# The second feed-forward product by Strassen's seven block products, with its rows kept in HBM

## The chip, the cores and the metric

One core of a Trainium2 chip runs the whole kernel. The metric is the time of one execution on the device in microseconds (us), as the median of several runs. For one more execution there is a profile taken by the hardware profiler, with a trace of every instruction. TensorE multiplies matrices, VectorE and ScalarE work on whole tiles, GpSimd is a slower general engine that can also issue DMAs, and SyncE issues DMAs.

## The reference

One layer of a hybrid decoder for 1024 prompt rows and 8 sample rows, so 1032 rows of 1024 channels. After the mixer (projections, short convolution, state-space scan) and a first LayerNorm comes the feed-forward part, which is all that the change touches:

```
v = x * (1 + sc2) + sh2
hid = jnp.square(jax.nn.relu(jnp.einsum('bld,df->blf', v, w_up)))
x = layer_norm(ALPHA * x + (1 + g2) * jnp.einsum('blf,fd->bld', hid, w_down), ln2_g, ln2_b)
```

`w_up` is 1024 x 4096 and `w_down` 4096 x 1024, in float32. `g2` depends on the channel, and for the sample rows also on the row.

## The kernel before, in words

Everything lies transposed: a tile has 128 channels on the partitions and the 1032 rows along the free dimension. The hidden layer has 4096/128 = 32 such tiles, and the output has 8 (`x1[0]` to `x1[7]`, in SBUF).

Each float32 operand is split into a high part in fp32r and a low part (what the high part leaves), by a cast on ScalarE and a subtraction on VectorE (`split`, line 201). A product of two such operands takes three matmuls: high by high, low by high, high by low (`term`, line 204). `product` (line 212) makes one output tile from a list of operand tiles: for each of the three blocks of 344 rows it runs all terms into one PSUM bank and then calls an eviction. Line 210 is the matmul of every such product.

`hidden(i)` (line 949) makes hidden tile i from the eight tiles of v: 3 x 8 x 3 = 72 matmuls; its eviction is ReLU on ScalarE, a square on VectorE and the split (lines 944 and 945). The tiles are taken in five groups of four (`NFA`, line 985) and two of six (`NFB`, line 1002). After each group the down product adds what the group gives to all eight output tiles: for each of them, 3 blocks by 4 (or 6) hidden tiles by 3 matmuls, evicted by `gate_add` (line 786), one VectorE operation that multiplies PSUM by the gate and adds it to `x1[m]` in SBUF (line 789), with two small operations for the 8 sample rows (lines 792 and 793). In the last group the LayerNorm is worked in: the down product runs over blocks of 392, 384 and 256 rows (`LAST`), and statistics, normalisation and stores of one block lie beside the matmuls of the next.

Weights come in tiles of 512 KB (384 KB in the groups of six) through SyncE's queue, in the order of the list `order`, always one ahead of the tile in use, into two `raw` buffers, and are split into `whi` and `wlo`. The tile framework places each instruction in its engine's queue by a simulated schedule, puts in the semaphore waits, and hands out the buffers by tag. PSUM has four banks for products (`psm`) and three for small results (`pss`). GpSimd issues no DMA in this kernel; its descriptor space is set to 1024 bytes per partition (line 1188).

Of the kernel before, what the change touches and what calls it, by code (L numbers as in the profile page):

```python
# [10 lines left out]
F32 = mybir.dt.float32  # L11
# [6 lines left out]
P = 128  # L18
# [33 lines left out]
SLOTS = {"raw": 2, "whi": 2, "wlo": 2, "G": 2, "xg": 2, "yc": 2}  # L52


NFB = 2
NFA = (DFF // P - 6 * NFB) // 4

# [5 lines left out]
def cols(ap, b):  # L65
    return ap[:, b[0]:b[1]]


def build(tc, ctx, a):
# [23 lines left out]
    def tmp(w=T, dt=F32):  # L93
        return sp.tile([P, w], dt, tag="t", name=nm("t"), bufs=5)
# [46 lines left out]
    def part(tag, dt, w):  # L141
        return sp.tile([P, w], dt, tag=tag, name=nm(tag), bufs=SLOTS.get(tag, 1))
# [6 lines left out]
    def parts(raw, tags, w):  # L149
        hi, lo = (part(t, F32R, w) for t in tags)  # L150
        for ins, first in zip(split(raw, hi, lo), queue):
            after(ins, first)
        return hi, lo
# [8 lines left out]
    for b in range(NB):  # L162
        for m in range(8):
            if b and m % 2 == 0:
                continue
            order.append(("wout", 1, m) + ((("raw", f"S{m}", f"S{m + 1}"),) if m % 2 == 0 else ()))
    for f in range(NFA):
        order += [("wup", i) + ((("raw", "aw", "yt"),) if i == 2 else ()) for i in range(4 * f, 4 * f + 4)]
        order += [("wda", f, mp) for mp in range(4)]
    spare = [f"U{i}" for i in range(8, 14)] + ["C0", "C1", "C2", "C3", "G", "G"]  # L170
    for f in range(NFB):
        order += [("wup", 4 * NFA + 6 * f + i) for i in range(6)]
        for m in range(8):
            tags = ("raw", spare[2 * m - 4], spare[2 * m - 3])
            order.append(("wdb", f, m) + ((tags,) if f == NFB - 1 and m > 1 else ()))
    ahead = []

    queue = []
# [9 lines left out]
    def prefetch():  # L188
        if order:
            key, raw = load_next()  # L190
            ahead.append((key, parts(*raw)))

    def weights(*key):
        if not ahead:
            prefetch()
        got, w = ahead.pop(0)
        assert got == key, (got, key)
        prefetch()
        return w
# [12 lines left out]
    def product(w, ks, evac, blocks=BLOCKS):  # L212
        for b in blocks:
            ps = psm()
            for i, x in enumerate(ks):
                term(ps, w, x, i, len(ks), b)
            evac(b, ps[:, :b[1] - b[0]])
            if not quiet[0]:
                next(background, None)
# [499 lines left out]
    def pair(tags):  # L719
        return [slab(t, F32R) for t in tags]  # L720
# [228 lines left out]
    def hidden(i):  # L949
        w, evac, hl, _ = hidden_start(i)  # L950
        product(w, kv, evac)
        return hl
# [29 lines left out]
    for k in range(8):  # L982
        after(rescale(k, b), vcopy)

    for f in range(NFA):
        kh = [t[2] for t in two] if f == 0 else []
        kh += [hidden(4 * f + i) for i in range(len(kh), 4)]
        for mp in range(4):
            w = weights("wda", f, mp)
            for m in (2 * mp, 2 * mp + 1):  # L990
                product(w, [(4 * (m % 2) + i, h, l) for i, (h, l) in enumerate(kh)],
                        lambda b, ps: gate_add(x1[m], ps, M_G2, m, b))

    def row_shift():

        near, base = tmp(dt=F32R), tmp()
        nc.scalar.copy(near, x1[0])
        for b in BLOCKS:
            ln1.total(base, (cols(near, b),), P, b, w=rones)
        return base  # L1000

    for f in range(NFB):
        if f == NFB - 1:
            base = row_shift()
        kh = []
        for i in range(6):
            kh.append(hidden(4 * NFA + 6 * f + i))
            if f == NFB - 1:
                for m in ((0, 1), (2, 3, 4), (5, 6, 7), (), (), ())[i]:
                    tc.keep_in_program_order(tt(x1[m], x1[m], base, op=ALU.subtract))  # L1010
        kf = [(i, h, l) for i, (h, l) in enumerate(kh)]
        if f < NFB - 1:
            for m in range(8):
                product(weights("wdb", f, m), kf, lambda b, ps: gate_add(x1[m], ps, M_G2, m, b))
            continue
        total = ln1.total
        mean, rsum, qsum = (slab(t) for t in ("xg", "xg", "yc"))
        sq = {}

        def square(m, b):  # L1020
            sq[m] = cols(qsum if m == 0 else tmp(), b)
            act(sq[m], cols(x1[m], b), AF.Square)

        def add_x(m, b):
            s = cols(rsum, b)
            tt(s, s if m > 1 else cols(x1[0], b), cols(x1[m], b), op=ALU.add)

        def add_q(m, b):
            tt(cols(qsum, b), cols(qsum, b), sq[m], op=ALU.add)

        def moments(b, xs=(), qs=()):

            mu, s, q = cols(mean, b), cols(rsum, b), cols(qsum, b)
            total(mean, (s, *(cols(x1[m], b) for m in xs)), D, b)
            act(s, mu, AF.Square)
            total(qsum, (q, *(sq[m] for m in qs)), D, b, eps)

        def variance(b):
            s, q, w = cols(rsum, b), cols(qsum, b), cols(tmp(), b)
            tt(s, q, s, op=ALU.subtract)  # L1040
            act(q, s, AF.Ln)
            act(q, q, AF.Exp, scale=-0.5)
            act(w, q, AF.Square)
            return w

        def newton(b, w):
            s, q = cols(rsum, b), cols(qsum, b)
            stt(w, w, -0.5, s, op0=ALU.mult, op1=ALU.mult)
            stt(q, w, 1.5, q, op0=ALU.add, op1=ALU.mult)

        def center(m, b):
            tt(cols(x1[m], b), cols(x1[m], b), cols(mean, b), op=ALU.subtract)

        def affine(m, b, to):
            tt(cols(x1[m], b), cols(x1[m], b), cols(qsum, b), op=ALU.mult)  # L1055
            if m % 3 == 2:
                nc.gpsimd.tensor_scalar(to, cols(x1[m], b), vc(V_G2, m), vc(V_B2, m), op0=ALU.mult, op1=ALU.add)  # L1057
            else:
                act(to, cols(x1[m], b), AF.Identity, scale=vc(V_G2, m), bias=vc(V_B2, m))

        def output(m, b):
            affine(m, b, cols(x1[m], b))
            dma(a["o_y"][m, :, b[0]:b[1]], cols(x1[m], b))

        wd = []

        def down(m, b):
            product(wd[m], kf, lambda b, ps: gate_add(x1[m], ps, M_G2, m, b), (b,))
            square(m, b)

        b = LAST[0]
        for m in range(8):
            wd.append(weights("wdb", f, m))
            down(m, b)
            if m:
                add_x(m, b)
                add_q(m, b)
        moments(b)

        with tc.manual_schedule(engines={mybir.EngineType.DVE}):  # L1080
            for i in (1, 2):
                b, p, last = LAST[i], LAST[i - 1], i == 2
                for m in range(8):
                    down(m, b)
                    if m == 0:
                        center(0, p)
                        center(1, p)
                        w = variance(p)
                    elif m == 1:
                        center(2, p)  # L1090
                        newton(p, w)
                    else:
                        add_x(m - 1, b)
                        if not last or m < 7:
                            add_q(m - 1, b)
                        if m == 2:
                            output(0, p)
                            output(1, p)
                        elif m < 7:
                            center(m, p)  # L1100
                            output(m - 1, p)
                if not last:
                    add_x(7, b)
                    center(7, p)
                    add_q(7, b)
                    moments(b)
                    output(6, p)
                    output(7, p)
            moments(b, (7,), (6, 7))
            y = [tmp(4 * (b[1] - b[0])).rearrange("p (m c) -> p m c", m=4) for i in range(2)]  # L1110
            output(6, p)
            center(7, p)
            output(7, p)
            for m in range(3):
                center(m, b)
            w = variance(b)
            for m in range(3, 6):
                center(m, b)
            newton(b, w)
            for m in range(8):  # L1120
                if m > 5:
                    center(m, b)
                affine(m, b, y[m // 4][:, m % 4])
                if m % 2:
                    dma(a["o_y"][m - 1:m + 1, :, b[0]:b[1]].rearrange("m p c -> p m c"), y[m // 4][:, m % 4 - 1:m % 4 + 1])
# [81 lines left out]
```

## Time and profile before

| what | value |
|---|---|
| median of 3 runs | 1575.5 us (1573.29 to 1575.7) |
| the profiled execution's own time | 1574.45 us |
| its span, first to last instruction | 1572.6 us |
| mean granted TensorE clock | 0.994 of full speed |
| instructions | 23959, of them 10058 matmuls |

A share is an engine's busy time over the span. The predicted and the measured time are of a whole execution; the rows are all of the profiled one.

### The profile page before, as it was taken

To read this page: it belongs to the slowest core of one execution; us is meant where nothing else is said; L and a number is where in the kernel's file an instruction comes from. 1 tells how busy PE (TensorE), PEld (TensorE's weight loads), DVE (VectorE), ACT (ScalarE), POOL (GpSimd) and SP (SyncE) were. 2 spreads that over 40 slices of the span, in tenths; PEclk is the share of its full clock that TensorE was granted. 3 is DMA by queue.
4 is the path that set the end of the run, shared out by engine and by line. 5 is a ranking of instruction groups with operands and counts; after the bars stand their busy time and mean duration, and the time that the engine had idled before them with its cause. 6 is when DMAs were issued, how large, how long until landed. Compare 5 with 4: busy or idle time off the path is not lost.

```text
span 1572.6 us, 23959 instructions
## 1 busy us (share of the span) xinstructions
PE 1541.8 (98%) x10058; PEld 1489.2 (95%) x10058; DVE 868.6 (55%) x1653; ACT 526.3 (33%) x805; POOL 169.0 (11%) x168
## 2 busy tenths in 40 slices
PE   6999999999999999999999999999999999999996
PEld 5899999999889999999999999999999999999995
DVE  4575556677876742636996444434343433335477
ACT  2553323323333353613577121121312213113334
POOL 0004222221211311100241000000000000000001
PEclk9999999999999999999999999999999999999998
DMA  9332344344343323412221111111111111111102
GB/s 366 114 118 94 108 132 141 118 140 132 135 151 128 119 96 108 175 42 93 82 68 54 41 54 41 48 47 42 53 41 54 41 54 34 45 56 51 61 31 88
DMA packets 49628, 141.44 MB, mean 90 GB/s; under 512 B 5736, under 2 KB 14696, under 8 KB 49520
## 3 DMA queue, kind: packets, MB, share of 16 engines
q1 hardware_dynamic: 49520, 139.91, 27.4%
q8 instruction: 79, 1.29, 0.3%
q14 instruction: 29, 0.24, 0.1%
HBM read 126.33 MB, written 13.56 MB: 89 GB/s over the span
## 4 chain that ended last, share of the span: by engine, by line
PE 94%; DVE 3%; DMA 1%; ACT 1%; issue 1%; POOL 0%; SPq 0%; ACTq 0%; DVEq 0%; POOLq 0%
PE mm L210 86%; PE ada L229 2%; PE sm L651 1%; PE sm L643 1%; PE sm L842 1%; PE sm L638 1%; PE sm L673 1%; PE sm L210 1%; DMA S<-in_xT 0%; PE sm L617 0%; DVE U L1055 0%; PE sm L236 0%; DMA s<-in_ssm 0%; PE sm L597 0%; PE mm L425 0%
## 5 line engine op out<-in xcount | busy, mean ns | idle before, releaser
L210 PE MATMUL mm<-U,whi 128*128 128x344 f32 x3058 | 778.5, 323 | 4.6 <-ACT U L336 4.6
L210 PEld LDWEIGHTS mm<-U,whi 128*128 128x128 f32 x3058 | 536.6, 188 | 21.4 <-issue 11.8
L210 PE MATMUL mm<-U,wlo 128*128 128x344 f32 x1529 | 488.1, 322 | 0.0
L202 ACT CAST whi<-raw 128x1024 fp32r<-128x1024 f32 (+1 forms) x122 | 125.7, 1030 | 544.0 <-PE mm L210 529.8
L210 PEld LDWEIGHTS mm<-U,wlo 128*128 128x128 f32 x1529 | 286.9, 188 | 3.0 <-issue 2.8
L789 DVE SCALAR_TENSOR_TENSOR U<-mm,mod,U 128x344 f32<-128x344 f32 (+3 forms) x216 | 122.7, 571 | 206.5 <-PE mm L210 206.5
L210 PE MATMUL mm<-S,whi 128*128 128x344 f32 (+3 forms) x912 | 232.8, 320 | 0.0
L202 DVE TENSOR_TENSOR wlo<-raw,whi 128x1024 fp32r<-128x1024 f32 (+1 forms) x122 | 146.5, 1201 | 132.2 <-ACT whi L202 131.8
L210 PEld LDWEIGHTS mm<-S,whi 128*128 128x128 f32 x912 | 160.6, 188 | 0.3
L210 PE MATMUL mm<-S,wlo 128*128 128x344 f32 (+3 forms) x456 | 145.3, 320 | 0.0
L210 PE MATMUL mm<-C,whi 128*128 128x344 f32 x516 | 143.0, 320 | 0.0
L944 DVE TENSOR_TENSOR t<-t 128x344 f32<-128x344 f32 x96 | 49.3, 515 | 87.5 <-ACT t L944 87.5
L210 PEld LDWEIGHTS mm<-C,whi 128*128 128x128 f32 x516 | 92.9, 188 | 0.1
L210 PEld LDWEIGHTS mm<-S,wlo 128*128 128x128 f32 x456 | 85.6, 188 | 0.1
L1057 POOL TENSOR_SCALAR U<-U,vec 128x392 f32<-128x392 f32 (+1 forms) x4 | 5.6, 1388 | 720.0 <-DVE U L1055 720.0
L210 PE MATMUL mm<-C,wlo 128*128 128x344 f32 x258 | 82.5, 320 | 0.0
L210 PE MATMUL mm<-G,whi 128*128 128x344 f32 x258 | 82.1, 321 | 0.1
L210 PE MATMUL mm<-xg,whi 128*128 128x344 f32 x258 | 82.0, 320 | 0.0
L387 DVE SCALAR_TENSOR_TENSOR t<-t,vec,t 128x1064 f32<-128x1064 f32 (+1 forms) x52 | 71.8, 1388 | 10.7 <-ACT t L385 9.7
L944 ACT ACTIVATE t<-mm 128x344 f32<-128x344 f32 x96 | 43.6, 455 | 97.0 <-PE mm L210 97.0
L210 PE MATMUL mm<-yc,whi 128*128 128x344 f32 x210 | 66.8, 322 | 0.0
L945 DVE TENSOR_TENSOR S<-t,S 128x344 fp32r<-128x344 f32 x66 | 33.9, 516 | 29.6 <-ACT S L944 29.3
(360 smaller groups left out, 2117.7 us busy)
## 6 DMA issues: line engine op xcount, KB each, us to landing
raw<-in_win SPq DMA_DIRECT2D x44, 512.0 KB, 3.7
aw<-in_wada SPq DMA_DIRECT2D x33, 512.0 KB, 4.2
raw<-in_wup SPq DMA_DIRECT2D x32, 512.0 KB, 3.5
raw<-in_wout SPq DMA_DIRECT2D x24, 512.0 KB, 3.5
raw<-in_wda SPq DMA_DIRECT2D x20, 512.0 KB, 3.5
G<-acd SPq DMA_DIRECT2D x16, 512.0 KB, 3.9
raw<-in_wdb SPq DMA_DIRECT2D x16, 384.0 KB, 3.1
S<-in_xT SPq DMA_DIRECT2D x8, 516.0 KB, 10.2
```

Source lines behind the costliest of these rows:

```text
L202: return nc.scalar.copy(thi, src), tt(tlo, src, thi, op=ALU.subtract)
L210: mm(ps[:, :b[1] - b[0]], wt, cols(xt, b), start=(i == 0 and q == 0), stop=(i == n - 1 and q == 2))
L229: mm(ps[32 * g:32 * g + 32, :256], cs[:, 2 * kp + k2, :], w[:, c:c + 256], start=(kp == 0), stop=(kp == KD // 2 - 1), tile_position=(0, 32 ...
L387: stt(r, t[:, k:k + n], wt(k), r, op0=ALU.mult, op1=ALU.add)
L638: mm(po[:, i * P:(i + 1) * P], st[:, h0:h0 + P], bc[2 + g][:, sl], start=True, stop=True)
L643: mm(py[r * HD:(r + 1) * HD, i * P:(i + 1) * P], xg[g][:, 0, h * HD:(h + 1) * HD], Gs[g][:, h, :], start=True, stop=True, tile_position=(0 ...
L651: mm(pst, bt[:, g * P:(g + 1) * P], xg[g][:, 1], start=True, stop=True)
L673: mm(pn[:, :BW], w, cols(src, b), start=(i == 0), stop=(i == len(srcs) - 1))
L789: stt(dst[:, lo:hi], ps[:, :hi - lo], mod[:, row + m, 0:1], dst[:, lo:hi], op0=ALU.mult, op1=ALU.add)
L842: mm(pn, w, src, start=(i == 0), stop=(i == len(srcs) - 1))
L944: return [lambda: act(x, ps, AF.Relu), lambda: tt(x, x, x, op=ALU.mult), lambda: nc.scalar.copy(xh, x), lambda: tt(xl, x, xh, op=ALU.subtr ...
L945: lambda: tt(xl, x, xh, op=ALU.subtract)]
```

## The change

Tiles 0 to 5 of the hidden layer go through the down product as a group of six before, into `x1` in SBUF; each `x1[m]` is then stored to a buffer `x1d[m]` in HBM. Tiles 26 to 31 are the last group of six, as before. The 20 tiles between them are taken in five groups of four. For a group, the down product of one pair of output tiles is a 2 x 2 block product: two pairs of hidden tiles by two output tiles by two sets of rows (the 1032 rows are seen as quarters of 258, and a set is two of them). It is computed by seven block products in place of eight, in Strassen's form as Winograd gave it: sums of weight blocks (`seven_parts`) and sums of hidden blocks (`operands`) are formed in SBUF by VectorE and then split. `seven` runs the products; one PSUM pair goes on accumulating through four of them and is read after each, so that each result is added to the rows that need it. The seven adds go to HBM: ScalarE copies one quarter and VectorE the other from PSUM, with the gate, to one of five SBUF buffers, and GpSimd issues a DMA that adds the buffer to the rows in HBM. After the last group the eight tiles are loaded back to SBUF. The cut diff (the list of weights and the host's layout of `w_down` follow it):

```diff
-NFB = 2
-NFA = (DFF // P - 6 * NFB) // 4
+NFS = 5
+NF = 6
+SPAIR = 0, 2, 1, 3
+QW = T // 4
...
+    def seven_parts(raw, n):
+        ha, la = part("whi", F32R, 768), part("wlo", F32R, 768)
+        sums, hb, lb = (part(f"U{t + n % 2}", dt, 1024) for t, dt in ((6, F32), (2, F32R), (4, F32R)))
+        a11, a12, a22, a21 = (raw[:, 256 * i:256 * i + 256] for i in range(4))
+        s1, s2, s3, s4 = (sums[:, 256 * i:256 * i + 256] for i in range(4))
+        for c in (0, 384):
+            split(raw[:, c:c + 384], ha[:, c:c + 384], la[:, c:c + 384])
+        tt(s1, a21, a22, op=ALU.add)
+        tt(s2, s1, a11, op=ALU.subtract)
+        tt(s3, a11, a21, op=ALU.subtract)
+        tt(s4, a12, s2, op=ALU.subtract)
+        for c in (0, 512):
+            split(sums[:, c:c + 512], hb[:, c:c + 512], lb[:, c:c + 512])
...
-    for f in range(NFA):
-        kh = [t[2] for t in two] if f == 0 else []
-        kh += [hidden(4 * f + i) for i in range(len(kh), 4)]
+    x1d = [dp.tile([P, T], F32, tag=f"x1d{m}", name=f"x1d{m}") for m in range(8)]
+    kh = [t[2] for t in two] + [hidden(i) for i in range(2, NF)]
+    kf = [(i, h, l) for i, (h, l) in enumerate(kh)]
+    for m in range(8):
+        product(weights("wdb", 0, m), kf, lambda b, ps: gate_add(x1[m], ps, M_G2, m, b))
+        dma(x1d[m], x1[m])
...
+    def hidden_raw(i):
+        r = tmp()
+        product(weights("wup", i), kv, lambda b, ps: act(cols(r, b), ps, AF.Relu))
+        tt(r, r, r, op=ALU.mult)
+        return r
...
+    def operands(j, ra, rb):
...
+        tt(t1, a4[:, :, 1], a4[:, :, 0], op=ALU.subtract)
+        tt(t3, b4[:, :, 1], a4[:, :, 1], op=ALU.subtract)
+        tt(t2, b4[:, :, 1], t1, op=ALU.subtract)
+        tt(t4, b4[:, :, 0], t2, op=ALU.subtract)
...
+            split(src, *hl)
...
+    evs = ["wb", "wc", "w0", "s0", "s0"]
+    def add_rows(ps, m, h):
+        tag = evs[0]
+        evs.append(evs.pop(0))
+        ev = sp.tile([P, 2, QW], F32, tag=tag, name=nm("ev"), bufs=2 if tag == "s0" else 1)
+        act(ev[:, 0], ps[0][:, :QW], AF.Copy, scale=mod[:, M_G2 + m, 0:1])
+        n = QW - NS if h else QW
+        ts(ev[:, 1, :n], ps[1][:, :n], mod[:, M_G2 + m, 0:1], None, op0=ALU.mult)
+        if h:
+            tt(ev[:, 1, n:], ps[1][:, n:QW], mod[:, M_G2 + m, 1:9], op=ALU.mult)
+        nc.gpsimd.dma_start(four(x1d[m])[:, :, h], ev, accum_op=ALU.add)
+    def seven(f, mp):
+        w = weights("wds", f, mp)
+        m1, m2 = 2 * mp, 2 * mp + 1
+        def multiply(ps, a_, b_, first=False):
+            for p in range(2):
+                for j in range(2):
...
+                    for q, (wt, xt) in enumerate(((wh, xh), (wl, xh), (wh, xl))):
+                        mm(ps[p][:, :QW], wt, xt, start=first and j == 0 and q == 0, stop=(j == 1 and q == 2),
+                           skip_group_check=not first)
+        one, other = [psm(), psm()], [psm(), psm()]
+        u, v = (other, one) if mp % 2 else (one, other)
+        y = [pss(), pss()]
+        multiply(u, "a11", "b11", True)
+        add_rows(u, m1, 0)
+        multiply(v, "s3", "t3", True)
+        add_rows(v, m2, 1)
+        multiply(u, "s2", "t2")
+        add_rows(u, m2, 0)
+        multiply(y, "a12", "b21", True)
+        add_rows(y, m1, 0)
+        multiply(u, "s1", "t1")
+        add_rows(u, m2, 1)
+        multiply(v, "a22", "t4")
+        add_rows(v, m2, 0)
+        multiply(u, "s4", "b22")
+        add_rows(u, m1, 1)
+    first = hidden_raw(NF)
+    for f in range(NFS):
+        n = NF + 4 * f
+        rb = hidden_raw(n + 2)
+        operands(0, first, rb)
+        ra = hidden_raw(n + 1)
+        rb = hidden_raw(n + 3)
+        operands(1, ra, rb)
+        if f < NFS - 1:
+            first = hidden_raw(n + 4)
+        else:
+            kh = [hidden(n + 4)]
         for mp in range(4):
-            w = weights("wda", f, mp)
-            for m in (2 * mp, 2 * mp + 1):
-                product(w, [(4 * (m % 2) + i, h, l) for i, (h, l) in enumerate(kh)],
-                        lambda b, ps: gate_add(x1[m], ps, M_G2, m, b))
+            seven(f, mp)
+    for m in range(8):
+        x1[m] = slab(f"U{m}")
+        dma(x1[m], x1d[m])
...
```

The row shift (the subtraction of a common base from `x1`) moves with the last group and stays between its up products, of which the first is now made before the last four calls of `seven`.

## Rows read from the trace of the kernel before

**Rows 1.** The page's head: span, and busy time, share and instructions by engine
```profile
span 1572.6 us, 23959 instructions
PE 1541.8 (98%) x10058; PEld 1489.2 (95%) x10058; DVE 868.6 (55%) x1653; ACT 526.3 (33%) x805; POOL 169.0 (11%) x168
```
**Rows 2.** The page's 40 slices: TensorE's busy tenths and granted clock
```profile
PE   6999999999999999999999999999999999999996
PEclk9999999999999999999999999999999999999998
```
**Rows 3.** The page's chain that ended last, by engine
```profile
PE 94%; DVE 3%; DMA 1%; ACT 1%; issue 1%; POOL 0%; SPq 0%; ACTq 0%; DVEq 0%; POOLq 0%
```
**Rows 4.** Timeline of SyncE's queue, DMA issues: start us, us, what
```profile
883.65 34.40 SPq L146 DMA_DIRECT2D raw<-in_wup  x4
929.11 34.41 SPq L146 DMA_DIRECT2D raw<-in_wda  x4
974.55 34.31 SPq L146 DMA_DIRECT2D raw<-in_wup  x4
...
1247.06 57.06 SPq L146 DMA_DIRECT2D raw<-in_wup  x6
```
**Rows 5.** Busy time in a window: us, PE, PEld, DVE, ACT, POOL; PEclk, DMA, GB/s
```profile
895.00:1404.00 509.00, 509.00 (x3229) 509.00 (x3228) 201.52 (x390) 107.30 (x179) 0.00 (x0) 1.00 0.15 47
```
**Rows 6.** Timeline of TensorE, the last block of 256 rows: start us, us, what
```profile
1535.58 0.28 PE L210 MATMUL mm<-S,whi 128*128 128x256 f32 x1
...
1539.86 0.52 PE L210 MATMUL mm<-S,U 128*128 128x256 f32 x3
```
**Rows 7.** Groups by line and shape: busy us, mean ns, then idle before
```profile
L789 DVE SCALAR_TENSOR_TENSOR U<-mm,mod,U 128x256 f32<-128x256 f32 x8 | 3.8, 479 | 0.0
L792 DVE TENSOR_TENSOR gs<-mm,mod 128x8 f32<-128x8 f32 x8 | 1.3, 157 | 0.0
L1026 DVE TENSOR_TENSOR xg<-xg,U 128x256 f32<-128x256 f32 x5 | 2.1, 416 | 0.0
L1026 DVE TENSOR_TENSOR xg<-xg,U 128x384 f32<-128x384 f32 x6 | 3.3, 549 | 0.0
L202 DVE TENSOR_TENSOR wlo<-raw,whi 128x1024 fp32r<-128x1024 f32 x43 | 52.7, 1225 | 65.2 <-ACT whi L202 65.2
L944 DVE TENSOR_TENSOR t<-t 128x344 f32<-128x344 f32 x78 | 40.1, 515 | 75.9 <-ACT t L944 75.9
L944 ACT ACTIVATE t<-mm 128x344 f32<-128x344 f32 x78 | 35.4, 455 | 78.0 <-PE mm L210 78.0
```
**Rows 8.** DMA issues of whole rows: count, KB each, median us to landing
```profile
ycd<-yc SPq DMA_DIRECT2D x8, 516.0 KB, 3.1
U<-in_xT SPq DMA_DIRECT2D x8, 516.0 KB, 7.9
```
**Rows 9.** Busy time in a window, columns as in rows 5
```profile
1485.00:1500.00 15.00, 15.00 (x86) 15.00 (x85) 10.83 (x25) 6.16 (x9) 0.00 (x0) 1.00 0.41 132
```
**Rows 10.** SyncE's issue of a load (min/median/max ns), GpSimd's smallest arithmetic (group)
```profile
L146 SPq DMA_DIRECT2D raw<-in_wup x32: 327/328/328, 803.2 to 1440.4; - x32
L546 POOL TENSOR_TENSOR xdt<-xsm,ddx 128x4 f32<-128x4 f32 x16 | 9.1, 566 | 14.3 <-DVE xsm L580 6.8 <-ACT ddx L502 6.7
```
**Rows 11.** DMA issues of 256 KB, columns as in rows 8
```profile
s<-in_ssm SPq DMA_DIRECT2D x16, 256.0 KB, 4.7
o_ssm<-s SPq DMA_DIRECT2D x16, 256.0 KB, 4.4
o_y<-t SPq DMA_DIRECT2D x4, 256.0 KB, 2.3
```

More of the change, by code (lines that the diff above doesn't have):

```diff
@@ L166, in build, with up @@
             order.append(("wout", 1, m) + ((("raw", f"S{m}", f"S{m + 1}"),) if m % 2 == 0 else ()))
-    for f in range(NFA):
-        order += [("wup", i) + ((("raw", "aw", "yt"),) if i == 2 else ()) for i in range(4 * f, 4 * f + 4)]
-        order += [("wda", f, mp) for mp in range(4)]
-    spare = [f"U{i}" for i in range(8, 14)] + ["C0", "C1", "C2", "C3", "G", "G"]
[L171 to L175, printed above, removed]
+    def up(i):
+        return [("wup", i) + ((("raw", "aw", "yt"),) if i == 2 else ())]
+    for i in range(NF):
+        order += up(i)
+    order += [("wdb", 0, m) for m in range(8)]
+    order += up(NF)
+    for f in range(NFS):
+        for i in SPAIR[1:]:
+            order += up(NF + 4 * f + i)
+        order += up(NF + 4 * f + 4)
+        order += [("wds", f, mp) for mp in range(4)]
+    for i in range(1, NF):
+        order += up(NF + 4 * NFS + i)
+    spare = [f"U{i}" for i in range(8, 14)] + ["C0", "C1", "C2", "C3", "G", "G"]
+    for m in range(8):
+        tags = ("raw", spare[2 * m - 4], spare[2 * m - 3])
+        order.append(("wdb", 1, m) + ((tags,) if m > 1 else ()))
     ahead = []
@@ L190, in prefetch @@
             key, raw = load_next()
-            ahead.append((key, parts(*raw)))
+            ahead.append((key, parts(*raw) if key[0] != "wds" else seven_parts(raw[0], key[2])))
+    def seven_parts(raw, n):
[11 more added lines that the diff above has]
+            split(sums[:, c:c + 512], hb[:, c:c + 512], lb[:, c:c + 512])
+        blocks = [(ha, la, i) for i in range(3)] + [(hb, lb, i) for i in range(4)]
+        return {k: (h[:, 256 * i:256 * i + 256], l[:, 256 * i:256 * i + 256])
+                for k, (h, l, i) in zip(("a11", "a12", "a22", "s1", "s2", "s3", "s4"), blocks)}
     def weights(*key):
@@ L983, in build @@
         after(rescale(k, b), vcopy)
-    for f in range(NFA):
-        kh = [t[2] for t in two] if f == 0 else []
-        kh += [hidden(4 * f + i) for i in range(len(kh), 4)]
-        for mp in range(4):
-            w = weights("wda", f, mp)
-            for m in (2 * mp, 2 * mp + 1):
-                product(w, [(4 * (m % 2) + i, h, l) for i, (h, l) in enumerate(kh)],
-                        lambda b, ps: gate_add(x1[m], ps, M_G2, m, b))
[L994 to L1015, printed above, removed]
+    x1d = [dp.tile([P, T], F32, tag=f"x1d{m}", name=f"x1d{m}") for m in range(8)]
@@ new lines, in build, with four @@
+    kh = [t[2] for t in two] + [hidden(i) for i in range(2, NF)]
[3 more added lines that the diff above has]
+        dma(x1d[m], x1[m])
+    def four(t):
+        return t.rearrange("p (a h c) -> p a h c", a=2, h=2)
+    def hidden_raw(i):
[3 more added lines that the diff above has]
+        return r
@@ new lines, in build @@
+    sops = {}
+    def operands(j, ra, rb):
+        if j == 0:
+            sops["b11"] = pair(("S0", "S1"))
+        a4, b4 = four(ra), four(rb)
+        for x, o in zip(sops["b11"], (0, 1)):
+            x2 = x[:, 2 * QW * j:2 * QW * j + 2 * QW].rearrange("p (a c) -> p a c", a=2)
+            if o == 0:
+                nc.scalar.copy(x2, a4[:, :, 0])
+                bh = x2
+            else:
+                tt(x2, a4[:, :, 0], bh, op=ALU.subtract)
+        ta, tb = tmp(), tmp()
+        t1, t3, t2, t4 = four(ta)[:, :, 0], four(ta)[:, :, 1], four(tb)[:, :, 0], four(tb)[:, :, 1]
+        tt(t1, a4[:, :, 1], a4[:, :, 0], op=ALU.subtract)
+        tt(t3, b4[:, :, 1], a4[:, :, 1], op=ALU.subtract)
+        tt(t2, b4[:, :, 1], t1, op=ALU.subtract)
+        tt(t4, b4[:, :, 0], t2, op=ALU.subtract)
+        for src, names, tags in ((rb, ("b21", "b22"), (("S2", "S3"), ("U14", "U15"))),
+                                 (ta, ("t1", "t3"), (("S4", "S5"), ("yt", "st"))),
+                                 (tb, ("t2", "t4"), (("S6", "S7"), ("U0", "U1")))):
+            hl = pair(tags[j])
+            split(src, *hl)
+            for h, name in enumerate(names):
+                sops[name, j] = [four(t)[:, :, h] for t in hl]
@@ new lines, in seven @@
+    def seven(f, mp):
[4 more added lines that the diff above has]
+                for j in range(2):
+                    wh, wl = (t[:, j * P:(j + 1) * P] for t in w[a_])
+                    if b_ == "b11":
+                        xh, xl = (t[:, (2 * j + p) * QW:(2 * j + p + 1) * QW] for t in sops["b11"])
+                    else:
+                        xh, xl = (t[:, p] for t in sops[b_, j])
+                    for q, (wt, xt) in enumerate(((wh, xh), (wl, xh), (wh, xl))):
[18 more added lines that the diff above has]
+        add_rows(u, m1, 1)
@@ new lines, in build @@
+    first = hidden_raw(NF)
+    for f in range(NFS):
+        n = NF + 4 * f
[6 more added lines that the diff above has]
+            first = hidden_raw(n + 4)
+        else:
+            kh = [hidden(n + 4)]
+        for mp in range(4):
+            seven(f, mp)
+    for m in range(8):
+        x1[m] = slab(f"U{m}")
+        dma(x1[m], x1d[m])
+    near, base = tmp(dt=F32R), tmp()
@@ L1016, in build @@
+    nc.scalar.copy(near, x1[0])
+    for b in BLOCKS:
+        ln1.total(base, (cols(near, b),), P, b, w=rones)
+    for i in range(1, NF):
+        kh.append(hidden(NF + 4 * NFS + i))
+        for m in ((0, 1), (2, 3, 4), (5, 6, 7), (), ())[i - 1]:
+            tc.keep_in_program_order(tt(x1[m], x1[m], base, op=ALU.subtract))
+    kf = [(i, h, l) for i, (h, l) in enumerate(kh)]
+    if ks:
         total = ln1.total
@@ L1072, in build @@
         for m in range(8):
-            wd.append(weights("wdb", f, m))
+            wd.append(weights("wdb", 1, m))
             down(m, b)
@@ L1165 @@
     a["wup"] = c_(g["w_up"][0].reshape(KD, P, 32, P).transpose(2, 1, 0, 3)).reshape(32, P, 1024)
-    wd, cut = g["w_down"][0], 4 * NFA * P
-    a["wda"] = c_(wd[:cut].reshape(NFA, 4, P, 4, 2, P).transpose(0, 3, 2, 4, 1, 5)).reshape(NFA, 4, P, 1024)
-    a["wdb"] = c_(wd[cut:].reshape(NFB, 6, P, 8, P).transpose(0, 3, 2, 1, 4)).reshape(NFB, 8, P, 768)
+    wd = g["w_down"][0].reshape(32, P, 8, P)
+    ends = np.stack([wd[:NF], wd[32 - NF:]])
+    a["wdb"] = c_(ends.transpose(0, 3, 2, 1, 4)).reshape(2, 8, P, NF * P)
+    mid = wd[NF:32 - NF].reshape(NFS, 2, 2, P, 4, 2, P)
+    mid = np.stack([mid[:, h, :, :, :, m] for h, m in ((0, 0), (1, 0), (1, 1), (0, 1))])
+    a["wds"] = c_(mid.transpose(1, 4, 3, 0, 2, 5)).reshape(NFS, 4, P, 1024)
     a["vec"] = c_(np.concatenate(
```

## The prediction
> **What bounds the kernel now.** I read the head of the page first: 1572.6 us of span with TensorE busy for 98% of it, VectorE for 55%, ScalarE for 33%, GpSimd for 11% [rows 1]. [...] The chain of waits then puts 94% of the span on TensorE [rows 3]. A matmul taken out in the feed-forward stage therefore pays its full price, as long as nothing else starts to make TensorE wait. The issues of the weight loads on SyncE give the length of that stage: the loads for four feed-forward tiles begin at 883.65 us and again every 90.85 us until 1247.06 us, four periods in 363.41 us [rows 4]. One period is 288 up and 288 down matmuls of 344 columns (the down half: 8 output tiles by 3 blocks by 12), so 157.7 ns each, and the down half costs 45.43 us. In the 509 us from 895 us TensorE is busy for all 509, VectorE for 201.5 (40%), ScalarE for 107.3, and GpSimd for none [rows 5].
>
> **The change, part by part.** The sum is made against the profiled execution's own 1574.45 us, which lies 1.05 us (0.07%) under the median of the runs.
>
> Matmuls. One call of the seven products makes 7 x 2 x 2 x 3 = 84 matmuls of 258 columns; four calls replace the 288 of 344 columns. Columns fall to 7/8, but the price is per matmul too, so I want the pace of a narrow one. The last stage has 256-column ones: from the start at 1535.58 to the one at 1539.86 lie 36, 118.9 ns each [rows 6]. From 157.7 ns at 344, one column costs (157.7 - 118.9)/88 = 0.44 ns, so 258 columns cost 119.8 ns. Four calls: 336 x 119.8 = 40.25 us. Saved: 45.43 - 40.25 = 5.18 us in each of five periods, **-25.9 us**. The twelve tiles outside keep their matmuls: six now come first, six last, at 18 per block as before.
>
> Evictions. Before, one VectorE operation of 344 columns added PSUM to the row in SBUF. Now ScalarE copies one quarter and VectorE another, seven times per call, and TensorE comes back to the same banks after 12 matmuls (1.44 us). VectorE's nearest row is the 256-column one from PSUM, 0.48 us, with 0.16 us more for eight sample columns in three of seven; ScalarE's is 0.46 us for 344 columns [rows 7]. Slack 0.8 us, if VectorE is free. It is not always: one call also splits 1024 weight columns into sums. By the widths shown (0.42 us at 256, 0.55 at 384, 1.22 at 1024, so 0.69 at 512) that is 2 x 0.55 + 4 x 0.42 + 2 x 0.69 = 4.2 us, and with 7 x 0.48 + 3 x 0.16 = 3.8 us for evictions VectorE is busy 8.0 of every 10.06 us [rows 7]. An eviction queued behind one such operation still arrives in time, behind two it does not. Per call I take 0.25 us, between 0 and 2.1 (0.3 us on each of seven): **+5 us**, ends 0 and +42.
>
> Operands. Before the seven products VectorE forms the second half of the sums: square 1.23, five operations of 516 columns at 0.70 (between 0.52 at 344 and 1.22 at 1024), three splits of 1032 at 1.23, and the first weight block's 4.2, together 12.6 us against 72 matmuls of the next tile, 11.4 us [rows 4, 7]. Late by 1.3 us at worst, but the first product needs only the first split. I take 1 us a period, **+5 us**, ends 0 and +13. The squares, now 1032 wide, lie under the up products, like the rest of the sums.
>
> Rows in HBM. Eight stores of 516 KB lie beside the first six tiles' down product (3.1 us each to landing [rows 8]). Eight loads come back after the last product, at 7.9 us each when queued together [rows 8]; SyncE must wait for the accumulations and for the U buffers, with the weight loads behind it. Five up products of 11.4 us cover them; I take 0, and without that cover it would cost up to about 20 us. The shift of the rows moves with them and stays under the same products.
>
> Accumulating transfers. They are the term on which the sign hangs. 28 in a period, 258 KB each, two runs of 1032 bytes per partition, fed from only five buffers: so 23 must have landed by the time that the products end, and TensorE is not held up while 23 spacings fit in 40.25 us, **1.75 us each**. The gain is gone when 23 spacings exceed that by 3.2 us (16/5), at 1.89 us. Before has no such transfer. From below: the DMA engines moved 132 GB/s at 0.41 of their time [rows 9], 322 GB/s at full share, 0.82 us for 264 KB moved once and 1.64 us if the read of the destination doubles it; the weights' 512 KB per call add 1.6 us to ten, partly beside. SyncE needs 0.33 us to issue one DMA, GpSimd 0.57 us for a four-column operation [rows 10]; writing 256 runs should cost more. From above: one at a time, each spacing is a whole landing. A store of 256 KB in 1 KB runs lands in 2.3 us, one among other traffic in 4.4, a load of 256 KB before it in 4.7, so 2.3 to 7.0 us [rows 11]. An eviction that waits for a buffer holds up the casts behind it on ScalarE and the weight sums behind it on VectorE, and TensorE needs both. If several are in flight, I take 1.5 us, nearest to the doubled engine time, and **0** for the end.
>
> [...]
>
> Sum: 1574.45 - 25.9 + 5 + 5 = 1558.6, **1559 us**.
>
> **The rivals.** *One at a time (slower).* The kernel leaves GpSimd's DMA queue 1024 bytes per partition (line 1188), and the fourth, fifth and sixth adds of a call go to rows that the first, second and third still write. If each transfer is issued only when the one before has landed, the five buffers fill and TensorE waits in every call. It decides from a spacing of 1.89 us. At 2.3 us a period's products take 52.9 us, 12.7 more, five times 63: 1622 us; at 4.4 us 101.2, five times 61: 1863 us; at 7.0 us beyond 2100. For it speaks the scratch size, unchanged since nothing used it; against it, that two other adds lie between any two on the same rows.
> [...]
>
> *GpSimd's issue limits (slower, less).* Several in flight, but 1.9 to 2.6 us to write one transfer's runs: 23 x 2.2 = 50.6, 10.3 over, five times 52: about 1610 us. For it: GpSimd needs 0.57 us for four columns; against: it has nothing else to do.
>
> *VectorE takes over.* The 42 us end of the evictions: 1574.45 - 25.9 + 5 + 42 = about 1596 us. For it 8.0 of 10.06 us; against: 2 us in every ten stay free, and a wait needs two operations ahead of an eviction.
>
> *It does not do what it says.* If a 258-column matmul fell off the pace of the 256-column one, by 7.7 ns each the gain halves: 1680 x 7.7 ns = 13 us, 1572 us. No row is against or for it beyond two columns' distance.
>
> **How the numbers follow.** Forecast 0.54 (1548 to 1571); about equal, from halved gain or small waits, 0.06; one at a time 0.21, GpSimd's issue 0.12, VectorE 0.07. One measurement of this kernel can tell about 0.2%, 3 us, from no change. Faster 0.54, same 0.06, slower 0.40. The forecast's own range is 1548 (all 25.9 us) to 1571. For 8 in 10 the range goes on through the two milder rivals and the quick end of the first, to 1720; above lies most of one at a time (0.18). It is the low end that the likeliest case holds.
>
> **What would show it.** Right: the products' stretches at about 40 us per four calls, TensorE at 9 in every slice, GpSimd transfers spaced under 1.75 us, VectorE near 65% in the stage. Wrong: TensorE idle in the seven products with an eviction as releaser, and that eviction waiting for the landing of a transfer (one at a time, or issue, told apart by whether the next issue follows the landing); TensorE waiting for VectorE that is busy (VectorE); a longer start-to-start at 258 columns; TensorE waiting at the end for the rows' load.

## The result: 1929 us, slower by a fifth

The changed kernel takes 1928.72 us (median of 4 runs, 1927.82 to 1933.89), beside 1575.08 us for the kernel before on the same chip: 1.2254 times as long (95% interval 1.223 to 1.2278). The forecast was 1559 us and its range ended at 1720.

The page of the changed kernel, its head, three rows of the slices (TensorE, its clock, the DMA engines), and the chain by engine:

```profile
span 1931.0 us, 25332 instructions
PE 1627.4 (84%) x10298; PEld 1554.2 (80%) x10298; DVE 938.9 (49%) x1773; ACT 611.2 (32%) x985; POOL 323.0 (17%) x308
...
PE   7999999999999999999996478459459647845996
...
PEclk9999999999999999999997678779669767976998
DMA  8233443444423413211315553553554555356312
...
PE 65%; issue 22%; POOL 5%; DMA 4%; DVE 2%; ACT 1%; SPq 0%; POOLq 0%; ACTq 0%; DVEq 0%
```

Up to slice 21 TensorE is at 9 as in [rows 2]. Then come five dips, one for each group of four hidden tiles, and between them it is at 7 to 9. The DMA engines are at about 5 there, so they are not full. The chain of waits, 94% TensorE in [rows 3], now has 22% of "issue": time in which an engine waited for nothing that the profile shows. The waits say whose:

```profile
ACT ev L1068 <- DMA x1d<-ev: 470.8, 85, 13.9
DVE ev L1070 <- DMA x1d<-ev: 449.5, 65, 12.7
POOL x1d L1073 <- issue: 375.8, 100, 7.1
...
PE mm L1088 <- ACT ev L1068: 212.4, 57, 9.3
...
PE mm L239 <- ACT ev L1068: 34.6, 9, 8.1
```

The columns are us in total, times, and the longest. Read from the bottom. TensorE waits 212 us for evictions on ScalarE in the seven products (line 1088), and 35 us even in the up products (line 239). ScalarE and VectorE wait for the landing of an adding transfer, because the buffer that they want to fill is still being read. GpSimd, which issues these transfers, waits 375.8 us, a hundred times, for nothing shown. Its timeline in one group:

```profile
1082.72 1.11 POOL L1073 DMA_DIRECT2D x1d<-ev  x1 [3.49 <-issue]
1087.41 1.10 POOL L1073 DMA_DIRECT2D x1d<-ev  x1 [3.58 <-issue]
1091.97 1.11 POOL L1073 DMA_DIRECT2D x1d<-ev  x1 [3.46 <-issue]
...
1148.90 1.11 POOL L1073 DMA_DIRECT2D x1d<-ev  x1 [3.73 <-ACT t L1029]
1183.17 1.10 POOL L1073 DMA_DIRECT2D x1d<-ev  x1 [33.17 <-DVE ev L1070]
```

Fifteen issues lie between 1082.72 and 1148.90: fourteen spacings of 4.73 us, each 1.10 us of issue and some 3.6 us of standing still. A transfer lands 4.4 us after its issue (median of 140), so each one starts when the one before has landed. SyncE's queue gives the length of a period, as in [rows 4]:

```profile
1148.85 33.65 SPq L148 DMA_DIRECT2D raw<-in_wds  x4
...
1312.59 33.67 SPq L148 DMA_DIRECT2D raw<-in_wds  x4
```

That is 163.74 us, against 90.85 before. The 28 spacings of a period make 132.4 us; with the idle stretch of 33.17 us in place of a usual 3.6 they make 162. Over the stretch 1037 to 1150 us TensorE is busy for 65.83 of 113 us at a mean granted clock of 0.66, where [rows 5] had 1.00. The clock fell with the idle time: from 1055 to 1060 us, with TensorE busy for 1.92 us, it is at its lower level, 0.50, and from 1150 to 1183 us, with TensorE busy throughout, at the upper, 1.00. What set the pace there was the spacing of the adds, which hardly moves: from 1188.88 to 1312.52 us, in the next group, 26 spacings are 4.76 us each.

### The profile page after: what moved, and what is told of

Same layout as the page of the kernel before. It is cut to its first block, busy times and chain, and to the rows that moved or that the text cites. A ratio compares the mean times of both kernels' runs of the same rounds, so it can differ in the third digit from the quotient of the medians.

```text
span 1931.0 us, 25332 instructions
## 1 busy us (share of the span) xinstructions
PE 1627.4 (84%) x10298; PEld 1554.2 (80%) x10298; DVE 938.9 (49%) x1773; ACT 611.2 (32%) x985; POOL 323.0 (17%) x308
## 3 DMA queue, kind: packets, MB, share of 16 engines
q0 software_dynamic: 38080, 37.00, 16.9%
## 4 chain that ended last, share of the span: by engine, by line
PE 65%; issue 22%; POOL 5%; DMA 4%; DVE 2%; ACT 1%; SPq 0%; POOLq 0%; ACTq 0%; DVEq 0%
PE mm L239 57%; POOL x1d L1073 5%; DMA x1d<-ev 3%; PE ada L258 1%; PE sm L680 1%; PE sm L672 1%; PE sm L871 1%; PE mm L1088 1%; PE sm L667 1%; PE sm L702 1%; PE sm L239 0%; PE sm L1088 0%; DMA raw<-in_win 0%; PE sm L646 0%; DVE U L1180 0%
## 5 line engine op out<-in xcount | busy, mean ns | idle before, releaser
L1073 POOL DMA_DIRECT2D x1d<-ev x140 | 154.6, 1104 | 816.5 <-issue 375.8
L1088 PE MATMUL mm<-S,U 128*128 128x258 f32 x480 | 116.6, 365 | 171.7 <-ACT ev L1068 161.9
L1070 DVE TENSOR_SCALAR ev<-mm,mod 128x250 f32<-128x250 f32 (+1 forms) x120 | 55.9, 478 | 398.5 <-DMA x1d<-ev 375.2
L1088 PEld LDWEIGHTS mm<-S,U 128*128 128x128 f32 x480 | 94.5, 260 | 183.0 <-ACT ev L1068 172.6
L231 ACT CAST whi<-raw 128x1024 fp32r<-128x1024 f32 (+2 forms) x142 | 123.1, 880 | 361.5 <-PE mm L239 348.6
L231 DVE TENSOR_TENSOR wlo<-raw,whi 128x1024 fp32r<-128x1024 f32 (+2 forms) x142 | 142.5, 1015 | 146.6 <-ACT whi L231 146.2
L1068 ACT ACTIVATE ev<-mm,mod 128x258 f32<-128x258 f32 x120 | 55.8, 475 | 433.7 <-DMA x1d<-ev 398.4
L1088 PE MATMUL mm<-S,whi 128*128 128x258 f32 x240 | 71.6, 349 | 53.0 <-ACT ev L1068 50.5
L1088 PEld LDWEIGHTS mm<-S,whi 128*128 128x128 f32 x240 | 54.7, 247 | 56.8 <-ACT ev L1068 54.1
L239 PE MATMUL mm<-yc,whi 128*128 128x344 f32 x210 | 71.1, 342 | 34.6 <-ACT ev L1068 34.6
L818 DVE SCALAR_TENSOR_TENSOR U<-mm,mod,U 128x344 f32<-128x344 f32 (+3 forms) x96 | 54.5, 570 | 91.0 <-PE mm L239 91.0
```

Source lines behind the costliest of these rows:

```text
L231: return nc.scalar.copy(thi, src), tt(tlo, src, thi, op=ALU.subtract)
L239: mm(ps[:, :b[1] - b[0]], wt, cols(xt, b), start=(i == 0 and q == 0), stop=(i == n - 1 and q == 2))
L818: stt(dst[:, lo:hi], ps[:, :hi - lo], mod[:, row + m, 0:1], dst[:, lo:hi], op0=ALU.mult, op1=ALU.add)
L1068: act(ev[:, 0], ps[0][:, :QW], AF.Copy, scale=mod[:, M_G2 + m, 0:1])
L1070: ts(ev[:, 1, :n], ps[1][:, :n], mod[:, M_G2 + m, 0:1], None, op0=ALU.mult)
L1073: nc.gpsimd.dma_start(four(x1d[m])[:, :, h], ev, accum_op=ALU.add)
```

## The experiments

The kernel before was timed again beside each set of kernels: 1575.38 us beside those on descriptor space, the plain store and the missing transfer, 1573.97 beside those with long runs and with adds to other rows, 1574.78 beside those with four adds, with a sixth buffer and 2048 bytes, and with the sums on GpSimd, 1574.6 beside the two that take sixth buffer and space alone. Ratios are to these.

**Descriptor space.** My theory after the result: the 1024 bytes that the kernel leaves for GpSimd's descriptors hold one such transfer and no second. The first two experiments change that number and nothing else; the instructions of every engine keep their order.

```diff
-    nc = bacc.Bacc("TRN2", target_bir_lowering=False, num_devices=1, dynamic_dma_scratch_size=1024)
+    nc = bacc.Bacc("TRN2", target_bir_lowering=False, num_devices=1, dynamic_dma_scratch_size=2048)   # second kernel: 4096
```

> The changed kernel with 2048 instead of 1024 bytes per partition for GpSimd's DMA descriptors; nothing else, and the same order on every engine. [...] Rival (the queue of GpSimd runs one transfer at a time whatever the space): spacing 4.7 us, 1929 us as before. [...]

With 4096 bytes:

> [...] Descriptor space: no add waits for space any more; the spacing is set by GpSimd's 1.1 us of issue and by the waits on the same rows, 1.1 to 1.5 us, the time 1550 to 1580 us. One at a time whatever the space: 1929 us.

Measured: 1654.57 us with 2048 bytes (1.0506, interval 1.0484 to 1.0527) and 1650.14 us with 4096 (1.0482, 1.0465 to 1.05). GpSimd's wait for nothing, with 2048 bytes and then with 4096:

```profile
POOL x1d L1073 <- issue: 41.2, 27, 4.0
```
```profile
POOL x1d L1073 <- issue: 23.2, 12, 4.7
```

From 375.8 us it falls to 41 and 23, and with 2048 bytes 274 of the 354 us of loss are gone. GpSimd now issues several adds in a row; one such place with 2048 bytes:

```profile
1139.91 3.35 POOL L1073 DMA_DIRECT2D x1d<-ev  x3 [6.25 <-ACT ev L1068]
```

The landings in the traces say how many adds are under way. In the changed kernel none of the 140 issues began before every earlier add had landed; with 2048 bytes at most two earlier ones were still under way when an issue began, with 4096 at most three. So the strict one-at-a-time was the descriptor space. The rest is something else, since twice the space gives only 4 us more. A window of the kernel with 4096 bytes (columns as in [rows 5]) in which 28 adds are issued:

```profile
1121.00:1185.00 64.00, 51.85 (x374) 50.60 (x373) 24.32 (x58) 19.11 (x40) 30.96 (x28) 0.92 1.00 152
```

The DMA engines are at 1.00, and they move only 152 GB/s; [rows 9] had 132 GB/s at 0.41. The adds come 64/28 = 2.29 us apart. The queue's row of the page (packets, MB, share of 16 engines' span) prices one of them, first in the changed kernel, then with 4096 bytes:

```profile
q0 software_dynamic: 38080, 37.00, 16.9%
```
```profile
q0 software_dynamic: 38080, 37.00, 17.8%
```

Share by span by 1/140: 0.169 x 1931.0/140 = 2.33 us of all sixteen engines per add in the one, 0.178 x 1643.6/140 = 2.09 us in the other. GpSimd itself is busy for 31 of the 64 us, 1.11 us per issue, so it isn't the limit.

**Without the addition, and without the transfer.** Two kernels at 1024 bytes whose output is not the layer's: one stores each result over the rows in place of adding it, one leaves the transfer out.

```diff
-        nc.gpsimd.dma_start(four(x1d[m])[:, :, h], ev, accum_op=ALU.add)
+        nc.gpsimd.dma_start(four(x1d[m])[:, :, h], ev)      # first kernel; the second has no such line
```

> The changed kernel at 1024 bytes, its transfers plain stores in place of adds (the sums in HBM are left out: each store overwrites the rows). [...] One at a time whatever the space or kind: near 1929 us, with a landing of 2.3 us at least 1700 us.

> The changed kernel without the 140 transfers (what the Strassen part gives is left out of the result; matmuls, evictions and operands stay). The prediction without its transfer term: 1558.6 us, between 1548 and 1600 us; about 40 us for four calls of the seven products and the clock at the upper level throughout. If VectorE's order or the operands hold TensorE up more than I took, more than 1575 us.

Measured: 1576.4 us with the plain store and 1550.45 us without the transfer (one run each). The queue of the plain stores, then SyncE's timeline without transfers, and two windows of that kernel: mostly under the up products, and over the four calls of the seven products, which begin at 1103.89 us:

```profile
q0 software_dynamic: 11200, 37.00, 6.7%
```
```profile
1072.34 33.67 SPq L148 DMA_DIRECT2D raw<-in_wds  x4
1158.26 33.68 SPq L148 DMA_DIRECT2D raw<-in_wds  x4
```
```profile
1074.00:1114.00 40.00, 40.00 (x275) 40.00 (x274) 28.83 (x49) 18.11 (x33) 0.00 (x0) 1.00 0.17 50
1104.00:1144.00 40.00, 40.00 (x334) 39.94 (x333) 23.16 (x55) 19.74 (x41) 0.00 (x0) 1.00 0.18 54
```

A plain store of the same bytes takes 0.067 x 1574.6/140 = 0.75 us of the engines, so the addition costs 2.8 times a store, not twice. It also makes 38080/140 = 272 packets where the store makes 80. The plain stores still cost 26 us, although the engines have time for them: each lands 3.5 us after its issue, and ScalarE waits 71.2 us for buffers that they hold. The space may have a part in this: at most two earlier stores were under way when one was issued, and GpSimd waits 54.4 us, 29 times, for nothing shown. No run gives the plain stores more space. Without transfers a period is 85.92 us, where the prediction's parts give 45.43 + 40.25 = 85.68; TensorE is busy for all of both windows, with ScalarE's and VectorE's evictions in place. The 334 matmuls of the second (all but four of them with 258 columns) come 119.8 ns apart. VectorE is busy for 23.16 of those 40 us, and for 28.83 in the first window, where the sums of hidden blocks are formed. Everything but the transfers therefore costs what the matmuls were forecast to cost, and nothing more.

**Longer runs.** If an add's engine time, and its share of the descriptor space, went by its number of runs, one run of 2064 bytes per partition in place of two of 1032 should halve both: from 2.1 us to about 1.1, with three adds under way in 1024 bytes as before in 2048. The rows in HBM are put in another order, in which a set of rows is one run; the space is 1024 bytes in the first kernel and 4096 in the second:

```diff
-        return t.rearrange("p (a h c) -> p a h c", a=2, h=2)
+        return t.rearrange("p (h a c) -> p a h c", a=2, h=2)
...
-        nc.gpsimd.dma_start(four(x1d[m])[:, :, h], ev, accum_op=ALU.add)
+        nc.gpsimd.dma_start(x1d[m][:, 2 * QW * h:2 * QW * h + 2 * QW], ev.rearrange("p a c -> p (a c)"), accum_op=ALU.add)
```

> [...] Theory (descriptor entries, and DMA-engine time by runs): three adds fit again, the engine time of one add falls from 2.1 us to about 1.1 us, GpSimd's issue below 1.1 us: 1550 to 1570 us. If the engine time goes by bytes: 2.1 us stay, time as with more space, 1640 to 1660 us. If the queue's space was not what held the adds at 1024 bytes: above 1700 us.

> The same with 4096 bytes. Theory: no more than a few us under the run at 1024 bytes, 1548 to 1565 us, and faster than the kernel before (1575 us). By bytes: 1640 to 1655 us.

Measured: 1645.72 us at 1024 bytes (1.0451, 1.0427 to 1.0474) and 1641.83 us at 4096 (1.043, 1.0415 to 1.0446). At 1024 bytes this does as much as doubling the space did: with half the runs more than one transfer fits (here too at most two earlier adds were under way at an issue). But the second limit hardly moves. At 4096 bytes, the queue's row and GpSimd's wait for landings:

```profile
q0 software_dynamic: 20160, 37.00, 15.8%
```
```profile
POOL x1d L1073 <- DMA x1d<-ev: 108.7, 33, 7.4
```

0.158 x 1639.9/140 = 1.85 us per add, from 2.09, though the packets are nearly halved (144 for 272). The forecast by runs was wrong: of the engines' time most goes by bytes, or by the addition itself. And GpSimd now waits 108.7 us for the landing of an earlier add to the same rows.

**Adds to the same rows.** In the kernel with 4096 bytes the fourth, fifth and sixth add of a call go to a second copy of the rows, which nothing reads (its eight first stores are added, and the output lacks these three results).

```diff
-    def add_rows(ps, m, h):
+    def add_rows(ps, m, h, to=x1d):
...
-        nc.gpsimd.dma_start(four(x1d[m])[:, :, h], ev, accum_op=ALU.add)
+        nc.gpsimd.dma_start(four(to[m])[:, :, h], ev, accum_op=ALU.add)
...
-        add_rows(y, m1, 0)
+        add_rows(y, m1, 0, x1e)      # so also the next two, (u, m2, 1) and (v, m2, 0)
```

> At 4096 bytes with the short runs of the changed kernel, but the fourth, fifth and sixth add of a call go to a second copy of the rows, so that no add waits for an earlier one of its call (the two copies are not joined: this part of the sum is left out; eight more stores fill the second copy). Theory (the DMA engines are full at 2.1 us per add): as at 4096 bytes, 1635 to 1655 us. Rival (the waits on the same rows set the pace there): 1560 to 1600 us.

Measured: 1617.38 us (one run), between what the two theories gave. It is 33 us under the kernel with the waits, so these matter; and it is still 67 us over the kernel without transfers, with 0.175 x 1615.3/140 = 2.02 us of the engines per add and evictions still waiting for buffers. Both, then, and neither alone.

**Fewer adds.** If it is the engines' time and the buffers, fewer adds must cure it. The first, second and third result stay in their buffers, and VectorE adds the fourth, fifth and sixth to them from PSUM; GpSimd issues four adds per call in place of seven. The layout is the one of long runs, the space 1024 bytes.

```diff
+            stt(ev[:, 0], ps[0][:, :QW], g, ev[:, 0], op0=ALU.mult, op1=ALU.add)
+            stt(ev[:, 1, :n], ps[1][:, :n], g, ev[:, 1, :n], op0=ALU.mult, op1=ALU.add)
...
-        add_rows(u, m1, 0)
+        e1 = add_rows(u, m1, 0, out=False)      # so also e2 and e3
...
-        add_rows(y, m1, 0)
+        add_rows(y, m1, 0, e1)                  # so also with e2 and e3
```

> At 1024 bytes with long runs; the fourth, fifth and sixth result of a call are added in SBUF to the buffers of the first, second and third by VectorE (PSUM times gate plus buffer, both quarters), so that only four adds per call go to HBM, each to rows of its own. Theory (the DMA engines are the second limit, 1.85 to 2.1 us per add): 16 adds take 30 to 34 us of 40.25, they fit; no waits on the same rows; VectorE goes from 8.0 to 9.5 of 10.06 us per call: 1552 to 1580 us. If GpSimd's queue or the waits for five buffers held the time: above 1600 us. If VectorE takes over: 1580 to 1620 us, with TensorE waiting for a busy VectorE.

Measured: 1571.08 us (10 runs, 1566.25 to 1575.11), 0.9974 (0.9961 to 0.9987): 3.7 us faster than before, all the same only a seventh of the 25.9 us that the matmuls were to give. 16 adds of 0.092 x 1564.1/80 = 1.80 us are 28.8 us of the engines per period, which 40 us cover. What is left, TensorE's first wait and ScalarE's behind it, from the profiled execution, the fastest of the ten:

```profile
PE mm L1099 <- ACT ev L1071: 10.1, 8, 2.3
...
ACT ev L1071 <- DMA x1d<-ev: 32.2, 12, 4.1
```

A buffer is now held from the first result to the landing of its add, and five are too few. The next kernel gives a sixth and 2048 bytes. Its tag, `s0`, is that of a tile of the mixer, which so gets a third buffer too:

```diff
-        s0 = sp.tile([P, HB, NST], F32, tag="s0", name=nm("s0"), bufs=2)
+        s0 = sp.tile([P, HB, NST], F32, tag="s0", name=nm("s0"), bufs=3)
...
-    evs = ["wb", "wc", "w0", "s0", "s0"]
+    evs = ["wb", "wc", "w0", "s0", "s0", "s0"]
...
-            ev = sp.tile([P, 2, QW], F32, tag=tag, name=nm("ev"), bufs=2 if tag == "s0" else 1)
+            ev = sp.tile([P, 2, QW], F32, tag=tag, name=nm("ev"), bufs=3 if tag == "s0" else 1)
...
-    nc = bacc.Bacc("TRN2", target_bir_lowering=False, num_devices=1, dynamic_dma_scratch_size=1024)
+    nc = bacc.Bacc("TRN2", target_bir_lowering=False, num_devices=1, dynamic_dma_scratch_size=2048)
```

> The same with 2048 bytes of descriptor space and a sixth buffer. Theory: a few us less than the run before where its buffers were short, 1551 to 1572 us, faster than the kernel before (1575 us).

Measured: 1556.24 us, 0.9878 (0.9861 to 0.9894). The two parts were then made alone:

> Four adds per call, five buffers, 2048 bytes of descriptor space (the sixth buffer left out). Theory: with adds of one run per row and only four per call the space no longer binds, and what was left in the run with 1024 bytes was the wait for a buffer, so the time stays near 1571 us, within 1565 to 1575. Rival: the space is what the sixth-buffer run gained from; then 1556 us, within 1553 to 1560.

> Four adds per call, six buffers, 1024 bytes of descriptor space. Theory: the sixth buffer alone gives what both gave, 1556 us, within 1553 to 1561. Rival: the space is what was gained from, and this stays at 1565 to 1575 us.

Measured: with the space alone 1573.67 us, 0.9992 (0.9979 to 1.0006); with the sixth buffer alone 1555.36 us, 0.9874 (0.9857 to 0.9891). The buffer gave all of it, the space nothing. TensorE's two longest waits, with the space alone and then with the buffer alone:

```profile
PE mm L1099 <- ACT ev L1071: 12.0, 7, 2.6
PE ada L258 <- DMA C<-in_wada: 5.5, 3, 5.1
```
```profile
PE ada L258 <- DMA C<-in_wada: 5.6, 3, 5.2
PE mm L239 <- ACT U L365: 3.7, 1, 3.7
```

The wait for an eviction is gone, and what is left lies in other stages. SyncE's timeline shows where the time was gained, first with five buffers and 1024 bytes, then with six:

```profile
1074.78 33.63 SPq L148 DMA_DIRECT2D raw<-in_wds  x4
1163.38 33.63 SPq L148 DMA_DIRECT2D raw<-in_wds  x4
```
```profile
1072.04 33.67 SPq L148 DMA_DIRECT2D raw<-in_wds  x4
1157.83 33.63 SPq L148 DMA_DIRECT2D raw<-in_wds  x4
```

A period is 88.60 us with five and 85.79 with six, as short as without transfers. The mixer gains nothing by its third buffer: the first load of up weights begins at 804.18 us in one and 803.92 in the other.

**A version that beats both.** To the six buffers and 2048 bytes the last kernel adds one thing: the sums of weight blocks go from VectorE to GpSimd, which has little to do.

```diff
-        tt(s1, a21, a22, op=ALU.add)
+        nc.gpsimd.tensor_tensor(s1, a21, a22, op=ALU.add)      # so also s2, s3, s4
```

> The same, with the four sums of weight blocks moved from VectorE to GpSimd (VectorE back to about 7.8 of 10.06 us per call, GpSimd at four issues of 0.9 us and four sums of about 1 us). If VectorE held TensorE up in the run before: 1550 to 1560 us. If GpSimd's issues now queue behind its sums: slower than the run before.

Measured: 1549.42 us (1548.47 to 1552.07), 0.984 (0.9825 to 0.9854), a little under the range expected. It is 25.4 us faster than the kernel before (1574.78), and beside the 1550.45 us without any transfer. Its page:

```profile
span 1547.1 us, 25161 instructions
PE 1515.2 (98%) x10298; PEld 1463.0 (95%) x10298; DVE 957.4 (62%) x1773; ACT 588.2 (38%) x925; POOL 319.4 (21%) x328
```

But it is not shown that VectorE had held TensorE up. One period of the kernel with six buffers and 2048 bytes, then one of this kernel:

```profile
1071.56:1157.35 85.79, 85.79 (x626) 85.79 (x626) 56.85 (x113) 31.85 (x56) 13.95 (x16) 1.00 0.48 99
```
```profile
1070.74:1156.60 85.86, 85.86 (x627) 85.86 (x626) 54.75 (x97) 31.79 (x56) 30.23 (x32) 1.00 0.50 99
```

TensorE is busy for all of both, and both last as long as a period without transfers: in the groups nothing was left to gain. The gain lies behind the start of the last group's weight loads (1328.90 and 1328.20 us): from there to the end of the span it is 225.7 and 218.9 us. In that stretch the rows come back from HBM, and line 1143 copies the first of them for the row shift:

```profile
ACT t L1143 <- DMA U<-x1d: 8.7, 1, 8.7
PE sm L871 <- ACT t L1143: 5.0, 1, 5.0
```
```profile
ACT t L1143 <- DMA U<-x1d: 5.4, 1, 5.4
PE sm L871 <- ACT t L1143: 0.9, 1, 0.9
```

The copy begins at 1411.44 us with the sums on VectorE and at 1404.71 with them on GpSimd, and from 1410 to 1430 us the granted clock was 0.91 in the first and 1.00 in the second. Why the rows come back earlier isn't shown; the last stage's instructions also stand in another order.

## Why the prediction was wrong

**The step that failed** is the last term of the sum, "Accumulating transfers", priced at 1.5 us a spacing "if several are in flight" and so at 0 for the end. It failed twice.

First, its condition was false. Several are not in flight: the spacing is 4.73 us, a whole landing and more. This is the rival *one at a time*, in its mechanism and its place (the 1024 bytes), and the price that it gave for 4.4 us, 1863 us, is 66 under what came. With 4.73 us its own formula gives 1901: 23 spacings are 108.8 us, 68.5 over the 40.25 us of products, 343 in five periods, on 1558.6. The rest is the count. I let five buffers drain under the up products, so that 23 spacings of 28 would count. From the kernel without transfers (1550.45 us) to 1928.72 it is 75.7 us a period, with the 40.25 of the products 115.9, and that is 24.5 spacings. The buffers don't drain quite freely: the up products wait for evictions too (TensorE's 34.6 us at line 239), 6.9 us a period, about the 1.5 spacings that came on top.

Second, 1.5 us would have been too low even with space for several: with 4096 bytes the engines' time alone is 2.1 us per add and the spacing 2.29 us, over the break-even of 1.89 us. I had chosen a value near the doubled engine time, 1.64 us, and the doubling was too small. The formula gives 1621 us for 2.29 (23 spacings are 52.7 us, 12.4 over, 62 in five periods), and with all 28 spacings 1678; 1650 came. So *GpSimd's issue limits* had, for this case, the spacing right and the cause wrong: no row stood behind its 1.9 to 2.6 us of writing, and an issue took 1.1 us.

**The chance** of 0.21 for one at a time was the real misjudgement. The price of "several in flight" had no row of the trace before behind it, and neither had "one"; both ends of the bound, 0.82 and 7.0 us, were known, and the break-even of 1.89 lay near the lower. With a sixth of the interval on the winning side I gave the win 0.54.

How much of the space one add takes is not shown. The runs show how many adds were under way, the new one included: one at 1024 bytes, up to three at 2048, up to four at 4096, and up to three at 1024 with half the runs.

**What held.** Matmuls: -25.9 us forecast, and the kernel without transfers is 24.9 us faster than the one before (1575.38 to 1550.45, one run), the best kernel 25.4; the 119.8 ns for 258 columns and the period of 85.92 us against 85.68 are as forecast. Evictions and operands: +5 us each forecast, together about 1, so the sum was some 8 us too high without the transfers. VectorE is busy for 23.16 of 40 us in the products, not for 8.0 of every 10.06, partly since three of a period's four sets of weight sums are formed under the up products, and *VectorE takes over* did not come. Rows in HBM: 0 forecast, and no wait of TensorE for them was seen in the kernel without transfers; with the adds in place TensorE waits behind their load for 5.0 us in one kernel and 0.9 in the best. *It does not do what it says* is refuted by the same period.

What stays open: how the time that is left with 4096 bytes splits between the engines' time, the waits of adds for earlier adds to the same rows, and the buffers. The runs show that each of the three counts, not how they add up.

## What to carry to other kernels

When a change moves work to a queue that the kernel has not used, look first at what the kernel has set aside for that queue, and take "one" as the base case until a trace shows two: 1024 bytes let one add be under way here, 2048 up to three. Price the transfer per buffer held: here longer runs, fewer adds and one buffer more turned a loss of a fifth into a gain of 19 us (1574.6 to 1555.36), while more descriptor space alone left a loss of 5%. An issuing engine that waits for nothing shown, at the pace of landings, was here the sign of full descriptor space (issues 4.73 us apart, landings after 4.4).

## What the runs showed of the hardware that was not expected

A DMA that adds to HBM took 2.8 times the DMA engines' time of one that stores the same bytes: 2.09 us against 0.75 for 258 KB. Halving its runs took off only 0.24 us. GpSimd's own issue depends on the form; minimum, median and maximum in ns of the add with two runs per partition (the changed kernel), the add with one, and the plain store:

```profile
L1073 POOL DMA_DIRECT2D x1d<-ev x140: 1088/1100/1259, 1019.3 to 1802.6; - x140
```
```profile
L1073 POOL DMA_DIRECT2D x1d<-ev x140: 853/876/1911, 1019.4 to 1499.8; - x140
```
```profile
L1073 POOL DMA_DIRECT2D x1d<-ev x140: 682/697/1002, 1019.5 to 1432.9; - x140
```

All of them are over twice SyncE's 0.33 us [rows 10]. And the waits for descriptor space had no releaser in these traces: they stood as "issue", 375.8 us at 1024 bytes and 41.2 at 2048.

VectorE gained little when GpSimd took the weight sums. Sixteen sums of 0.42 us left it in a period, 6.7 us, but its busy time fell only from 56.85 to 54.75. Two of its subtractions in that period of the last kernel, a sum on GpSimd beside them, and a sum while VectorE was idle:

```profile
1075.41 3.47 DVE L231 TENSOR_TENSOR S<-t,S 128x1032 fp32r<-128x1032 f32 x2
```
```profile
1076.05 1.74 POOL L213 TENSOR_TENSOR U<-U,raw 128x256 f32<-128x256 f32 x1
1087.28 0.74 POOL L213 TENSOR_TENSOR U<-U,raw 128x256 f32<-128x256 f32 x1
```

With the sums on VectorE such a subtraction took 1.23 us (mean of 15); beside GpSimd's sums it took about 1.7, and the sum itself 1.74 us in place of 0.74.
